# Pooling mixer of a hybrid encoder: folding counts, norm weight and scale into its matrices

## The chip, the cores and the metric

The kernel runs on one core of a Trainium2 chip. Its engines are TensorE (PE in the profile, with its weight loads as PEld), VectorE (DVE), ScalarE (ACT), GpSimd (POOL) and SyncE (SP); each takes its instructions from a queue of its own. The metric is device microseconds of one execution, lower is better.

## What is computed

Four encoder layers, each a token mixer and a SwiGLU feed-forward block with RMS norms before and after, on x of 256 tokens by 1024 channels, all in float32. The mixers are a gated convolution, a pooling mixer, attention, and a convolution again, so the order of sub-layers is conv, ffn, pool, ffn, attn, ffn, conv, ffn. The change is in the pooling mixer, whose four groups of 256 channels have windows of 2, 4, 8 and 16 tokens:

```python
def _pool_mixer(xn, w_pool, scale):
    ...
    for g, w in enumerate(POOL_WINDOWS):
        lo = jnp.maximum(t - w // 2, 0)
        hi = jnp.minimum(t + w - 1 - w // 2, s - 1)
        ...
        cnt = (hi - lo + 1).astype(jnp.float32)
        outs.append(win_sum / cnt[None, :, None] - xf[..., sl])
    p = jnp.stack(outs, axis=2)
    y = jnp.einsum('bsgc,gcd->bsgd', p, w_pool.astype(jnp.float32)).reshape(bsz, s, D_MODEL)
    return (y * scale.astype(jnp.float32)).astype(xn.dtype)

x = x + _rms(m, g[1])      # g[0] weighs the norm ahead of the mixer
```

## The kernel before

The 256 tokens are two tiles of 128 (t = 0 and 1). A float32 product is made of three matmuls of a reduced type (fp32r): every operand is split into hi, a rounded copy, and lo, the rest, and hi by hi, hi by lo and lo by hi are added up in PSUM. The split of a weight (class Weights, prep) is a ScalarE copy into hi and a VectorE subtraction into lo, in halves of 128x1024; weights come as raw tiles of 1 MB with SyncE's DMAs, three buffers deep, and up to 12 split halves are kept ahead of their use. W.pump(k) asks for k more halves at places in the program, W.get asks for one that is needed now. Activations are split the same way by split(): ScalarE copies, VectorE subtracts.

The wrapper Pinned keeps every instruction in program order on its engine, so an instruction whose data are late holds all behind it on that engine.

Each sub-layer ends in boundary(t), for one tile and then the other: ScalarE squares the result (junk) with a running sum, VectorE multiplies it by the gain of the norm behind (gpost, into mg), makes the reciprocal root (st) in small steps, adds to x, and, if the next sub-layer is not the mixer, multiplies by the gain of the norm ahead (gpre, into mg again). x_transposed(t) then transposes mg on TensorE into a PSUM bank tr and splits it into xh and xl. A feed-forward block begins with start(): a projection of tile 0 for slab 0, two steps of slab 1, x_transposed(1), the rest of slab 1, then the evacuation of both (ScalarE sg, VectorE h) and the transposes of the first h; then the projections of tile 1 follow, which need xh and xl of tile 1. A projection is 24 matmuls of 512 columns.

The gains gpost have one buffer: GpSimd issues the load of the next one when VectorE has read the last for the final time.

The pooling mixer needs no transposes ahead of it: boundary makes xh and xl in token order. pool_tables, called in run ahead of the feed-forward block before the mixer (i == 1), loads for each group a band matrix (1 in the window, minus the count on the diagonal) in two bandf buffers and casts it on GpSimd to bandr, and loads inv (one over the counts) and sc (the scale, broadcast). pool_mixer multiplies xh and xl by bandr into four PSUM banks (two of mm, two of tr), 256 columns each, with 24 calls of warm (matmuls of the identity, two instructions each, whose result nobody reads) between t = 0 and 1. Eight pieces of 128x256 are then weighted by the norm weight gc and split into ph and pl, and multiplied by the pool weight (raw tile 49) into acc: for each t, c outside and g inside. After 14 more warm calls VectorE multiplies acc by inv and sc into m, and boundary takes m.

Of the kernel before, what the change touches and what calls it, by code (L numbers as in the profile page):

```python
# [17 lines left out]
P = 128  # L18
D = 1024
# [35 lines left out]
class Weights:  # L55
# [3 lines left out]
    def __init__(self, kb, n):  # L59
        self.kb, self.n = kb, n  # L60
        self.loaded = self.prepped = self.released = 0
        self.raw, self.split, self.uses = {}, {}, {}

    def load(self):
        if self.loaded >= self.n:
# [9 lines left out]
    def prep(self):  # L75
        kb, (i, c) = self.kb, divmod(self.prepped, 2)
        while self.loaded <= i:
            self.load()
        raw = self.raw[i][:, c * 1024 : (c + 1) * 1024]
        hi = kb.wsp.tile([P, 1024], F32R, tag="hi", name=f"hi{i}_{c}")  # L80
        lo = kb.wsp.tile([P, 1024], F32R, tag="lo", name=f"lo{i}_{c}")
        n = 512 if i == 0 else 1024
        for a in range(0, 1024, n):
            sl = slice(a, a + n)
            kb.A.copy(hi[:, sl], raw[:, sl])
            kb.V.tensor_tensor(lo[:, sl], raw[:, sl], hi[:, sl].bitcast(F32), op=ALU.subtract)
        self.split[i, c] = (hi, lo)
        self.uses[i, c] = 0
        self.prepped += 1
        if c == 1:  # L90
            del self.raw[i]
            while self.loaded < min(self.n, i + 1 + NR):
                self.load()
# [16 lines left out]


class Kernel:
    def __init__(self, ctx, tc, x, w, gains, taps, pscale, lam, subg, rel, onehot, band, invc, gcol, out):
        self.tc, self.nc = tc, tc.nc
        nc = self.nc
        self.V, self.A, self.T = Pinned(tc, nc.vector), Pinned(tc, nc.scalar), Pinned(tc, nc.tensor)
        self.G, self.SP = Pinned(tc, nc.gpsimd), Pinned(tc, nc.sync)
        self.w, self.gains, self.taps, self.out = w, gains, taps, out
        self.pscale, self.lamv, self.subg, self.rel = pscale, lam, subg, rel
        self.onehot, self.band, self.invc = onehot, band, invc  # L120
        pool = lambda name, bufs=1, **k: ctx.enter_context(tc.tile_pool(name=name, bufs=bufs, **k))
        self.c = pool("c")
        self.wraw = pool("wraw", NR)
        self.wsp = pool("wsp", NP)
        self.gp = pool("gp", 1)
        self.st = pool("st", 12)
        ps = bass.MemoryType.PSUM
        self.ps_acc = pool("ps_acc", 4, space=ps)
        self.ps_mm = pool("ps_mm", 2, space=ps)
        self.ps_tr = pool("ps_tr", 2, space=ps)  # L130
        self.dram = pool("dram", 1, space=bass.MemoryType.DRAM)
        self.wi = 0
        self.W = Weights(self, w.shape[0])
        self.x = self.c.tile([P, 2, D], F32, name="x")
        xv = x.rearrange("(t p) d -> p t d", p=P)
        self.gc = self.c.tile([P, 2, 8], F32, name="gc")
        self.A.dma_start(out=self.gc, in_=gcol)
        self.gc, self.gcp = self.gc[:, 0, :], self.gc[:, 1, :]
        self.SP.dma_start(out=self.x[:, 0, :], in_=xv[:, 0, :])
        self.W.load()  # L140
        self.SP.dma_start(out=self.x[:, 1, :], in_=xv[:, 1, :])
        self.ident = self.c.tile([P, P], F32, name="ident")
        make_identity(nc, self.ident)
        self.xh = [self.c.tile([P, 8, P], F32R, name=f"xh{t}") for t in range(2)]
        self.xl = [self.c.tile([P, 8, P], F32R, name=f"xl{t}") for t in range(2)]
        self.r2 = [self.c.tile([P, 1], F32, name=f"rstd{t}") for t in range(2)]
        self.xg, self.s2 = [None, None], [None, None]
# [423 lines left out]

    def pool_tables(self, pool):

        G = self.G
        self.bandr = pool.tile([P, 4, 2, S], F32R, name="bandr")
        for g in range(4):
            bandf = pool.tile([P, 2, S], F32, tag="bandf", name="bandf", bufs=2)
            G.dma_start(out=bandf, in_=self.band[:, g])
            G.tensor_copy(self.bandr[:, g], bandf)
        self.inv = pool.tile([P, 2, 4], F32, name="inv")  # L580
        G.dma_start(out=self.inv, in_=self.invc)
        self.sc = pool.tile([P, D], F32, name="sc")
        G.dma_start(out=self.sc, in_=self.pscale[0].partition_broadcast(P))

    def pool_mixer(self, pool, g_post, g_pre, nxt):


        V, A, W, T = self.V, self.A, self.W, self.T
        wid = self.take(1)[0]
        banks = [self.mm(), self.mm(), self.tr(), self.tr()]  # L590
        spare = self.acc()
        for t in range(2):
            if t == 1:
                self.warm(spare, 24)
            for g in range(4):
                for c in range(2):
                    col = slice((2 * g + c) * P, (2 * g + c + 1) * P)
                    for k, xs in enumerate((self.xh[t], self.xl[t])):
                        T.matmul(
                            banks[g][:, c * S : (c + 1) * S], xs.rearrange("p c n -> p (c n)")[:, col],  # L600
                            self.bandr[:, g, t, :], start=t + c + k == 0, stop=t + c + k == 3,
                        )
        ph = pool.tile([P, 8, S], F32R, name="ph")
        pl = pool.tile([P, 8, S], F32R, name="pl")
        for c in range(2):
            for g in range(4):
                ch, b = 2 * g + c, banks[g][:, c * S : (c + 1) * S]
                gc = self.gcp[:, ch : ch + 1]
                A.activation(ph[:, ch, :], b, AF.Copy, scale=gc)
                V.scalar_tensor_tensor(pl[:, ch, :], b, gc, ph[:, ch, :].bitcast(F32), op0=ALU.mult, op1=ALU.subtract)  # L610
        accs = [[self.acc(), self.acc()] for _ in range(2)]
        for t in range(2):
            sl = slice(t * P, (t + 1) * P)
            for c in range(2):
                for g in range(4):
                    hi, lo = W.get(wid, g // 2)
                    o = accs[t][g // 2][:, (g % 2) * 256 : (g % 2 + 1) * 256]
                    ws = slice((2 * (g % 2) + c) * 256, (2 * (g % 2) + c + 1) * 256)
                    T.matmul(o, ph[:, 2 * g + c, sl], hi[:, ws], start=c + g % 2 == 0, stop=False)
                    T.matmul(o, ph[:, 2 * g + c, sl], lo[:, ws], start=False, stop=False)  # L620
                    T.matmul(o, pl[:, 2 * g + c, sl], hi[:, ws], start=False, stop=c + g % 2 == 2)
            for c in range(2):
                W.used(wid, c)
        self.warm(self.mm(), 14)
        for t in range(2):
            m = pool.tile([P, D], F32, tag="m", name="m", bufs=2)
            for g in range(4):
                mc = slice(g * 256, (g + 1) * 256)
                V.scalar_tensor_tensor(
                    m[:, mc], accs[t][g // 2][:, (g % 2) * 256 : (g % 2 + 1) * 256],  # L630
                    self.inv[:, t, g : g + 1], self.sc[:, mc], op0=ALU.mult, op1=ALU.mult,
                )
            self.boundary(t, [m[:, 0:512], m[:, 512:1024]], g_post, g_pre, nxt, 0 if t else None)
            if t == 0:
                self.x_transposed(0)
                W.pump(1)
# [284 lines left out]
def constants():  # L921
    rel = np.arange(-255, 257)
    n = np.abs(rel)
    bucket = np.searchsorted(np.array(BUCKET_STARTS), n, side="right") - 1 + np.where(rel > 0, 16, 0)
    onehot = (bucket[None, :] == np.arange(32)[:, None]).astype(np.float32)
    t = np.arange(S)
    band = np.zeros((4, S, S), np.float32)
    inv = np.zeros((4, S), np.float32)
    for g, w in enumerate(WINDOWS):
        lo, hi = np.maximum(t - w // 2, 0), np.minimum(t + w - 1 - w // 2, S - 1)  # L930
        cnt = hi - lo + 1
        s = t[:, None]
        band[g] = ((s >= lo) & (s <= hi)).astype(np.float32) - np.where(s == t[None, :], cnt[None, :], 0)
        inv[g] = np.float32(1) / cnt.astype(np.float32)
    inv = np.ascontiguousarray(inv.reshape(4, 2, P).transpose(2, 1, 0))
    band = np.ascontiguousarray(band.reshape(4, 2, P, S).transpose(2, 0, 1, 3))
    return onehot, band, inv


# [28 lines left out]
```

## Time and profile before

| | |
|---|---|
| median of 3 runs | 1116.5 us (1116.36 to 1116.82) |
| the profiled execution | 1116.26 us, of which the span is 1114.5 us |
| mean granted TensorE clock | 0.994 |
| busy, of the span | TensorE 98%, VectorE 62%, ScalarE 47%, GpSimd 2% |
| the first feed-forward block | starts at about 104 us |
| the pooling mixer | about 293 to 325 us |

A busy engine here is one that executes; waiting is not counted. Times within a trace are microseconds from the span's start. A row of the timeline gives start, duration, engine, line, operation, what is written from what is read, the shape, how many follow each other, and in brackets the idle time ahead of it with the engine that ended it. All instructions carry line 48, that of the wrapper, so one reads by the tiles' names.

### The profile page before, as it was taken

What the parts mean: (1) busy time and instruction counts of PE and PEld (TensorE: products, weight loads), DVE (VectorE), ACT (ScalarE), POOL (GpSimd) and SP (SyncE); (2) the same over time, 40 slices, a digit from 0 to 9 for tenths busy, and PEclk for the clock granted to TensorE, in tenths of its full rate; (3) what the DMA queues carried; (4) which work ended last, traced back from release to release, by engine and by line L of the source; (5) the groups of instructions that cost most, each with busy time, mean ns of one, the idle gap of its engine ahead of it and who ended that gap; (6) DMA issues with size and microseconds to landing.
All of it is one profiled execution on the core that took longest, in us unless ns stands there. A gap on an engine that the chain in (4) does not pass through costs nothing.

```text
span 1114.5 us, 12901 instructions
## 1 busy us (share of the span) xinstructions
PE 1089.4 (98%) x4974; PEld 886.4 (80%) x4974; DVE 692.2 (62%) x1147; ACT 529.0 (47%) x849; POOL 25.1 (2%) x45
## 2 busy tenths in 40 slices
PE   8999999999989999999998999999999999999997
PEld 6888888888868878888777778888888888888885
DVE  6867755454777554557676876455487777545443
ACT  6644544344446443445454564444355554534431
POOL 0000200000010001000000000000000000000000
PEclk9999999999989999999999999999999999999999
DMA  8754664554236557544533466454545644655421
GB/s 307 286 200 167 225 250 152 191 202 174 114 98 226 225 190 250 189 162 144 184 116 114 151 223 238 181 189 174 198 157 194 222 153 168 227 189 201 176 76 39
DMA packets 31086, 203.98 MB, mean 183 GB/s; under 512 B 3804, under 2 KB 4348, under 8 KB 7984
## 3 DMA queue, kind: packets, MB, share of 16 engines
q1 hardware_dynamic: 27216, 191.38, 46.9%
q0 software_dynamic: 3376, 11.25, 3.0%
q8 instruction: 39, 0.64, 0.2%
q10 hardware_dynamic: 432, 0.53, 0.1%
q14 instruction: 23, 0.19, 0.1%
HBM read 202.08 MB, written 2.11 MB: 183 GB/s over the span
## 4 chain that ended last, share of the span: by engine, by line
PE 90%; DVE 6%; ACT 2%; issue 1%; DMA 1%; SPq 0%; DVEq 0%; ACTq 0%
PE mm L48 58%; PE acc L48 28%; PE tr L48 4%; DVE st L48 2%; DVE lo L48 1%; DVE lg L48 1%; DVE x L48 1%; ACT hi L48 1%; ACT junk L48 1%; DVE mg L48 1%; DMA raw<-in_w 1%; ACT xh L48 1%; ACT lg L48 0%; DVE pl L48 0%; DVE xl L48 0%
## 5 line engine op out<-in xcount | busy, mean ns | idle before, releaser
L48 DVE TENSOR_TENSOR lo<-raw,hi 128x1024 fp32r<-128x1024 f32 (+1 forms) x364 | 426.0, 1219 | 64.0 <-ACT hi L48 63.3
L48 PE MATMUL mm<-hi,xh 128*128 128x512 f32 x992 | 398.5, 402 | 3.4 <-ACT hi L48 3.1
L48 PE MATMUL mm<-lo,xh 128*128 128x512 f32 x992 | 390.8, 394 | 1.7 <-DVE lo L48 1.7
L48 PE MATMUL mm<-hi,xl 128*128 128x512 f32 x992 | 391.0, 394 | 0.0
L48 ACT CAST hi<-raw 128x1024 fp32r<-128x1024 f32 (+1 forms) x364 | 359.3, 1051 | 11.1 <-DMA raw<-in_w 10.1
L48 PEld LDWEIGHTS mm<-hi,xh 128*128 128x128 f32 x992 | 187.3, 189 | 43.6 <-ACT hi L48 4.0
L48 PEld LDWEIGHTS mm<-lo,xh 128*128 128x128 f32 x992 | 187.7, 189 | 41.9 <-DVE lo L48 3.5
L48 PEld LDWEIGHTS mm<-hi,xl 128*128 128x128 f32 x992 | 187.1, 189 | 41.4 <-DVE xl L48 0.9
L48 ACT ACTIVATE sg<-mm,rstd 128x256 f32<-128x256 f32 x88 | 41.9, 476 | 362.0 <-PE mm L48 358.4
L48 DVE SCALAR_TENSOR_TENSOR h<-mm,rstd,sg 128x256 f32<-128x256 f32 x88 | 42.6, 484 | 264.7 <-ACT sg L48 264.7
L48 PE MATMUL acc<-hi,hh 128*128 128x512 f32 x352 | 117.0, 406 | 0.0
L48 PE MATMUL acc<-lo,hh 128*128 128x512 f32 x352 | 113.0, 395 | 0.0
L48 PE MATMUL acc<-hi,hl 128*128 128x512 f32 x352 | 113.0, 395 | 0.0
L48 PEld LDWEIGHTS acc<-lo,hh 128*128 128x128 f32 x352 | 66.2, 188 | 15.9
L48 PEld LDWEIGHTS acc<-hi,hl 128*128 128x128 f32 x352 | 66.1, 188 | 15.8
L48 PEld LDWEIGHTS acc<-hi,hh 128*128 128x128 f32 x352 | 63.3, 189 | 12.9 <-issue 0.9
L48 ACT ACTIVATE junk<-x 128x512 bf16<-128x512 f32 x32 | 20.2, 633 | 45.5 <-DVE x L48 45.4
L48 DVE TENSOR_TENSOR hl<-tr,hh 128x256 fp32r<-128x256 f32 x88 | 36.5, 415 | 2.3 <-ACT hh L48 2.3
L48 PEld LDWEIGHTS tr<-ident,h 128*128 128x128 f32 x176 | 24.5, 139 | 11.7
L48 PE MATMUL tr<-ident,h 128*128 128x128 f32 x176 | 33.4, 271 | 0.0
L48 ACT CAST hh<-tr 128x256 fp32r<-128x256 f32 x88 | 32.2, 366 | 2.5 <-PE tr L48 2.5
L48 ACT ACTIVATE junk<-acc 128x512 bf16<-128x512 f32 x28 | 16.7, 597 | 33.4 <-PE acc L48 33.4
(134 smaller groups left out, 636.7 us busy)
## 6 DMA issues: line engine op xcount, KB each, us to landing
raw<-in_w SPq DMA_DIRECT2D x180, 1024.0 KB, 4.8
gpost<-in_gains POOLq DMA_DIRECT2D x8, 512.0 KB, 4.1
gpre<-in_gains POOLq DMA_DIRECT2D x6, 512.0 KB, 5.0
x<-in_x SPq DMA_DIRECT2D x2, 512.0 KB, 6.3
bandf<-in_band POOLq DMA_DIRECT2D x4, 256.0 KB, 4.8
skew<-scr POOLq DMA_DIRECT2D x4, 256.0 KB, 5.4
bias<-skew POOLq DMA_DIRECT2D x4, 192.0 KB, 5.8
raw<-in_w SPq DMA_DIRECT2D x2, 256.0 KB, 4.5
```

The costliest lines, as they stand in the source:

```text
L48: r = f(*a, **k)
```

## The change

The band matrix now holds one over the count in the window, minus 1 on the diagonal, so that inv is gone; as such values are no longer exact in the reduced type, the band is split in two parts (bandh, bandl), and xh is multiplied by both, xl by bandh: 48 band matmuls in place of 32. The split is done by split(), a ScalarE copy and a VectorE subtraction for each group, where GpSimd cast. The load of sc comes first. The norm weight gcp and the scale sc are multiplied into the raw tile of the pool weight by VectorE (fold), four pieces of 128x256 for each half, ahead of that half's split. In the mixer the four PSUM banks are split whole, 128x512 each; the products go group by group; m is gone and boundary reads acc.

```diff
 # Weights.prep
         raw = self.raw[i][:, c * 1024 : (c + 1) * 1024]
+        if i in self.fold:
+            self.fold[i](raw, c)
 # pool_tables
-        self.bandr = pool.tile([P, 4, 2, S], F32R, name="bandr")
+        self.bandh = pool.tile([P, 4, 2, S], F32R, name="bandh")
+        self.bandl = pool.tile([P, 4, 2, S], F32R, name="bandl")
+        self.sc = pool.tile([P, D], F32, name="sc")
+        G.dma_start(out=self.sc, in_=self.pscale[0].partition_broadcast(P))
         for g in range(4):
             bandf = pool.tile([P, 2, S], F32, tag="bandf", name="bandf", bufs=2)
             G.dma_start(out=bandf, in_=self.band[:, g])
-            G.tensor_copy(self.bandr[:, g], bandf)
-        self.inv = pool.tile([P, 2, 4], F32, name="inv")
-        G.dma_start(out=self.inv, in_=self.invc)
-        self.sc = pool.tile([P, D], F32, name="sc")
-        G.dma_start(out=self.sc, in_=self.pscale[0].partition_broadcast(P))
+            self.split(bandf, self.bandh[:, g], self.bandl[:, g])
+
+        def fold(raw, half):
+            for j in range(4):
+                g, c = 2 * half + j // 2, j % 2
+                sl = slice(j * 256, (j + 1) * 256)
+                V.scalar_tensor_tensor(
+                    raw[:, sl], raw[:, sl], self.gcp[:, 2 * g + c : 2 * g + c + 1],
+                    self.sc[:, g * 256 : (g + 1) * 256], op0=ALU.mult, op1=ALU.mult,
+                )
+
+        self.W.fold[self.wi + 3 * NS] = fold
 # pool_mixer
-                for c in range(2):
-                    col = slice((2 * g + c) * P, (2 * g + c + 1) * P)
-                    for k, xs in enumerate((self.xh[t], self.xl[t])):
+                for k, (xs, band) in enumerate(((xh, self.bandh), (xh, self.bandl), (xl, self.bandh))):
+                    for c in range(2):
+                        col = slice((2 * g + c) * P, (2 * g + c + 1) * P)
                         T.matmul(
...
-        for c in range(2):
-            for g in range(4):
-                ch, b = 2 * g + c, banks[g][:, c * S : (c + 1) * S]
-                gc = self.gcp[:, ch : ch + 1]
-                A.activation(ph[:, ch, :], b, AF.Copy, scale=gc)
-                V.scalar_tensor_tensor(pl[:, ch, :], b, gc, ph[:, ch, :].bitcast(F32), op0=ALU.mult, op1=ALU.subtract)
+        for g in range(4):
+            f = lambda a: a[:, 2 * g : 2 * g + 2, :].rearrange("p c n -> p (c n)")
+            self.split(banks[g], f(ph), f(pl))
...
-            for c in range(2):
-                for g in range(4):
-                    hi, lo = W.get(wid, g // 2)
-                    o = accs[t][g // 2][:, (g % 2) * 256 : (g % 2 + 1) * 256]
+            for g in range(4):
+                hi, lo = W.get(wid, g // 2)
+                o = accs[t][g // 2][:, (g % 2) * 256 : (g % 2 + 1) * 256]
+                for c in range(2):
...
-            m = pool.tile([P, D], F32, tag="m", name="m", bufs=2)
-            for g in range(4):
-                mc = slice(g * 256, (g + 1) * 256)
-                V.scalar_tensor_tensor(
-                    m[:, mc], accs[t][g // 2][:, (g % 2) * 256 : (g % 2 + 1) * 256],
-                    self.inv[:, t, g : g + 1], self.sc[:, mc], op0=ALU.mult, op1=ALU.mult,
-                )
-            self.boundary(t, [m[:, 0:512], m[:, 512:1024]], g_post, g_pre, nxt, 0 if t else None)
+            self.boundary(t, accs[t], g_post, g_pre, nxt, 0 if t else None)
```

## Rows read from the trace of the kernel before

**Rows 1.** The page's busy shares: busy us, share of the span, instructions.
```profile
PE 1089.4 (98%) x4974; PEld 886.4 (80%) x4974; DVE 692.2 (62%) x1147; ACT 529.0 (47%) x849; POOL 25.1 (2%) x45
```
**Rows 2.** Timeline of TensorE behind the mixer, where the next block starts.
```profile
324.36 1.23 PE L48 MATMUL tr<-ident,mg 128*128 128x128 f32 x8 [2.26 <-DVE mg L48]
327.20 0.79 PE L48 MATMUL mm<-hi,xh 128*128 128x512 f32 x1 [1.62 <-ACT hi L48]
...
329.06 0.63 PE L48 MATMUL mm<-hi,xl 128*128 128x512 f32 x1
...
332.47 0.41 PE L48 MATMUL mm<-lo,xh 128*128 128x512 f32 x1
```
**Rows 3.** Timeline of TensorE, start of the first feed-forward block: transposes of h.
```profile
116.10 0.38 PE L48 MATMUL tr<-ident,h 128*128 128x128 f32 x2
```
**Rows 4.** Timeline of ScalarE there.
```profile
109.84 0.19 ACT L48 ACTIVATION_READ_ACCUMULATOR junk<-x 128x1 f32 x1
111.73 1.08 ACT L48 CAST xh<-tr 128x512 fp32r<-128x512 f32 x2 [1.70 <-PE tr L48]
```
**Rows 5.** Timeline of VectorE there.
```profile
114.92 0.48 DVE L48 SCALAR_TENSOR_TENSOR h<-mm,rstd,sg 128x256 f32<-128x256 f32 x1
```
**Rows 6.** Timeline of GpSimd there, and the landing times of the bandf loads.
```profile
108.71 0.54 POOL L48 DMA_DIRECT2D gpost<-in_gains  x1 [105.50 <-DVE mg L48]
109.25 0.54 POOL L48 DMA_DIRECT2D bandf<-in_band  x1
113.81 1.66 POOL L48 CAST bandr<-bandf 128x512 fp32r<-128x512 f32 x1 [4.03 <-DMA bandf<-in_band]
...
118.30 1.42 POOL L48 CAST bandr<-bandf 128x512 fp32r<-128x512 f32 x1 [2.33 <-DMA bandf<-in_band]
...
DMA to landing us min/median/max: 2.8/4.8/5.0
```
**Rows 7.** Windows there: stretch, us, POOL busy, PEclk, DMA share, GB/s.
```profile
111.00:112.00 1.00, 0.00 (x0) 1.00 1.19 274
...
122.00:123.00 1.00, 0.00 (x0) 1.00 1.06 451
```
**Rows 8.** Groups by form: count, busy us, mean ns, idle us before them.
```profile
L48 ACT CAST hi<-raw 128x512 fp32r<-128x512 f32 x4 | 2.3, 619 | 1.0 <-DMA raw<-in_w 1.0
L48 DVE TENSOR_TENSOR lo<-raw,hi 128x512 fp32r<-128x512 f32 x4 | 2.6, 689 | 1.0 <-ACT hi L48 1.0
```
**Rows 9.** Window behind the mixer: PE, PEld, DVE, ACT, POOL busy, PEclk, DMA, GB/s.
```profile
329.50:332.40 2.90, 2.90 (x8) 2.29 (x7) 1.58 (x3) 0.00 (x0) 0.00 (x0) 0.50 1.01 251
```
**Rows 10.** ScalarE's weight casts: the group until 240 us, then the timeline.
```profile
L48 ACT CAST hi<-raw x90: 614/1058/1107, 6.1 to 236.5; 128x1024 fp32r<-128x1024 f32 x86, 128x512 fp32r<-128x512 f32 x4
...
259.25 4.85 ACT L48 CAST hi<-raw 128x1024 fp32r<-128x1024 f32 x5
269.95 0.47 ACT L48 ACTIVATE sg<-mm,rstd 128x256 f32<-128x256 f32 x1 [5.85 <-PE mm L48]
...
270.57 1.06 ACT L48 CAST hi<-raw 128x1024 fp32r<-128x1024 f32 x1
275.68 0.47 ACT L48 ACTIVATE sg<-mm,rstd 128x256 f32<-128x256 f32 x1 [4.05 <-PE mm L48]
```
**Rows 11.** Timeline of VectorE at the mixer's end, t = 1.
```profile
317.36 1.66 DVE L48 SCALAR_TENSOR_TENSOR m<-acc,inv,sc 128x256 f32<-128x256 f32 x4
...
319.86 0.52 DVE L48 TENSOR_SCALAR st<-st 128x1 f32<-128x1 f32 x4 [0.25 <-ACT junk L48]
```
**Rows 12.** Timeline of TensorE in the mixer: band matmuls of t = 1, products, warm-ups.
```profile
301.23 0.38 PE L48 MATMUL mm<-bandr,xh 128*128 128x256 f32 x1 [0.73 <-ACT xh L48]
302.02 0.39 PE L48 MATMUL mm<-bandr,xl 128*128 128x256 f32 x1 [0.41 <-DVE xl L48]
...
303.85 0.28 PE L48 MATMUL acc<-hi,ph 128*128 128x256 f32 x1
...
309.76 3.29 PE L48 MATMUL mm<-ident 128*128 128x128 f32 x28
```

More of the change, by code (lines that the diff above doesn't have):

```diff
@@ L62, in __init__ @@
         self.raw, self.split, self.uses = {}, {}, {}
+        self.fold = {}
     def load(self):
@@ L112, with __init__ @@
 class Kernel:
-    def __init__(self, ctx, tc, x, w, gains, taps, pscale, lam, subg, rel, onehot, band, invc, gcol, out):
+    def __init__(self, ctx, tc, x, w, gains, taps, pscale, lam, subg, rel, onehot, band, gcol, out):
         self.tc, self.nc = tc, tc.nc
@@ L119, in __init__ @@
         self.pscale, self.lamv, self.subg, self.rel = pscale, lam, subg, rel
-        self.onehot, self.band, self.invc = onehot, band, invc
+        self.onehot, self.band = onehot, band
         pool = lambda name, bufs=1, **k: ctx.enter_context(tc.tile_pool(name=name, bufs=bufs, **k))
@@ L572, in pool_tables @@
     def pool_tables(self, pool):
-        G = self.G
-        self.bandr = pool.tile([P, 4, 2, S], F32R, name="bandr")
+        V, G = self.V, self.G
+        self.bandh = pool.tile([P, 4, 2, S], F32R, name="bandh")
+        self.bandl = pool.tile([P, 4, 2, S], F32R, name="bandl")
+        self.sc = pool.tile([P, D], F32, name="sc")
+        G.dma_start(out=self.sc, in_=self.pscale[0].partition_broadcast(P))
         for g in range(4):
@@ L594, in pool_mixer @@
                 self.warm(spare, 24)
+            xh, xl = (a[t].rearrange("p c n -> p (c n)") for a in (self.xh, self.xl))
             for g in range(4):
-                for c in range(2):
-                    col = slice((2 * g + c) * P, (2 * g + c + 1) * P)
-                    for k, xs in enumerate((self.xh[t], self.xl[t])):
+                for k, (xs, band) in enumerate(((xh, self.bandh), (xh, self.bandl), (xl, self.bandh))):
+                    for c in range(2):
+                        col = slice((2 * g + c) * P, (2 * g + c + 1) * P)
                         T.matmul(
-                            banks[g][:, c * S : (c + 1) * S], xs.rearrange("p c n -> p (c n)")[:, col],
-                            self.bandr[:, g, t, :], start=t + c + k == 0, stop=t + c + k == 3,
+                            banks[g][:, c * S : (c + 1) * S], xs[:, col], band[:, g, t, :],
+                            start=t + c + k == 0, stop=t + c + k == 4,
                         )
@@ L927, in constants @@
     band = np.zeros((4, S, S), np.float32)
-    inv = np.zeros((4, S), np.float32)
     for g, w in enumerate(WINDOWS):
         lo, hi = np.maximum(t - w // 2, 0), np.minimum(t + w - 1 - w // 2, S - 1)
-        cnt = hi - lo + 1
         s = t[:, None]
-        band[g] = ((s >= lo) & (s <= hi)).astype(np.float32) - np.where(s == t[None, :], cnt[None, :], 0)
-        inv[g] = np.float32(1) / cnt.astype(np.float32)
-    inv = np.ascontiguousarray(inv.reshape(4, 2, P).transpose(2, 1, 0))
+        inv = np.float32(1) / (hi - lo + 1).astype(np.float32)
+        band[g] = np.where((s >= lo) & (s <= hi), inv, np.float32(0)) - (s == t).astype(np.float32)
     band = np.ascontiguousarray(band.reshape(4, 2, P, S).transpose(2, 0, 1, 3))
-    return onehot, band, inv
+    return onehot, band
 def kernel(**inputs):
@@ L944 @@
     i = {k: np.asarray(v) for k, v in inputs.items()}
-    onehot, band, inv = constants()
+    onehot, band = constants()
     arrays = {
@@ L956 @@
         "band": band,
-        "invc": inv,
         "gcol": np.ascontiguousarray(i["norm_g"][0:2, 0].reshape(2, 8, P).transpose(2, 0, 1)),
```

## The prediction

> **What bounds the kernel now.** I read the page's busy shares first: TensorE is busy 98% of the span [rows 1]. The kernel is a row of matmuls with few holes, so a change is worth what it does to those holes. Next, what TensorE's matmuls wait for: at the pooling mixer the two longest waits are 2.26 us for mg and 1.62 us for a weight half, and the timeline puts both at its end, where the next feed-forward block starts [rows 2]. That is what the mixer's edits can win. The change also moves the band tables from GpSimd to ScalarE and VectorE, at the start of the feed-forward block before, around 110 us. So I read what those engines and TensorE do there [rows 3 to 6]: TensorE has no hole at all, and that is what the change can lose.
>
> **Part 1: the band tables, around 110 us.** pool_tables is called before ffn, so its instructions stand in each engine's order ahead of all of that block's. Before, only GpSimd was held: it loads a band, waits, casts it, loads the next, from 109.25 us on [rows 6], and nobody needs the result for another 180 us. After, each band is split by a ScalarE copy and a VectorE subtraction. The four copies stand on ScalarE behind the squares of the conv layer's last boundary (the last read-out ends at 109.84 + 0.19 = 110.03) and ahead of the copy xh of x_transposed(1), which starts at 111.73 [rows 4]; the four subtractions stand on VectorE ahead of xl and of h (114.92) [rows 5]. All engines keep program order, as before. So the first copy waits for a DMA that cannot be issued before gpost's (108.71, itself released by VectorE's last mg [rows 6]), and what queues behind it is xh, hi, sg on ScalarE and xl, lo, h on VectorE. TensorE waits for these: at 116.10 it is to transpose h [rows 3].
>
> When does ScalarE come free? GpSimd issues gpost at 108.71, now sc at 109.25, band 0 at 109.79 and band 1 at 110.33 (0.54 each [rows 6]). Before, band 0 was usable at 113.81, behind 512 KB of gpost. Now sc's 512 KB lie in front too. From 111 to 112 us the queues moved 274 GB/s, and they reach 451 nearby [rows 7]; 512 KB at some 340 GB/s, between these, are 1.5 us. So I take band 0 at 115.3 and band 1, 256 KB later, at 116.1. Bounds for band 0: 114.35 (sc costs nothing but its issue slot) and 116.2 (512 KB at the slower rate, and that slot). A copy of 128x512 costs 0.62 us and a subtraction 0.69 [rows 8], about 0.55 and 0.65 apart where they follow each other. There are two bandf buffers, so band 2 is issued when band 0's subtraction is done: 115.3 + 0.62 + 0.69 is about 116.6; band 3 at 117.4. The four band loads of before took 2.8 to 5.0 us to land, median 4.8; the 2.8 is band 1's, whose cast waited 2.33 us [rows 6], with nothing else moving. While ScalarE and VectorE stand still no raw buffer is released, so no weights are loaded, and I take 2.9; 5.0 is the other bound. Band 3 is then usable at 120.3 and its copy done at T = 120.95, with bounds 119.8 and 123.1.
>
> From there xh, xl, hi, lo, sg, h run as before: from xh's start (111.73) to h's end (114.92 + 0.48 = 115.40) is 3.67 us, and h was 0.70 us early for TensorE. The stall is T - 111.73 - 0.70 = T - 112.4, that is 8.5 us (7.4 to 10.7). Nothing covers it: TensorE's order has nothing else to issue. No second stall follows, as both engines' work behind xh is shifted as a whole, and slab 2, whose first half is the hi queued there, is needed only two projections (11 us) later.
>
> The Trainium skill (DMA: Bandwidth & Descriptors, Anatomy of one DMA) gives such a load a fixed 2.0 us plus its bytes at 436 GB/s, which is an estimate of 2.6 us for one band and 5.0 us for gpost, sc and band 0 together. By that rule T is 119.0, the stall 6.6 and the total 1122.9. The 2.8 us trip is near it; the median of 4.8 is not.
>
> **Part 2: the clock after that stall.** After the hole of 322.10 to 327.20, with eight transposes in it, the granted clock stood at 0.50, the 1.2 GHz level [rows 9], and 512-column matmuls came 0.427 us apart from 329.06 to 332.47 [rows 2] where 0.229 is usual: 8 matmuls, 1.6 us lost. Counted from 327.20 the slow stretch is 5.2 us, at half speed 2.6 lost. A hole of over 8 us should cost the like: I take 1.8 (1.4 to 2.6).
>
> **Part 3: the fold, and GpSimd.** Four VectorE products of 128x256 go ahead of each of the two casts of the pool weight, 1.7 us a half by the four m of the same form [rows 11]. This is raw 49, halves 98 and 99, so casts 101 and 102 (raw 0 has two casts more). Ninety casts are over by 240 us; then come 5, 1, 5, 1, so these are the last of the five at 259.25 and the one at 270.57 [rows 10]. The five end at 264.1, and ScalarE then idles until 269.95 (5.85 us idle): fold, cast and subtraction end near 269.1. The second ends near 275.3, the next sg follows at 275.68. Cost 0; without that cover each would delay an sg by up to 1.9 us. GpSimd loses four casts, one load and a wait: nothing is queued behind them until the gains of the mixer, so 0.
>
> **Part 4: the mixer.** Band matmuls grow from 32 to 48, 256 columns each, some 0.115 us apart. Those of t=0, 8 more, 0.93 us, lie ahead of the warm-ups; TensorE waited 0.73 us after these for xh at 301.23 [rows 12], and its short wait (0.26 us) among them for xl goes, since four xh products now stand first: cost 0 to 0.2. For t=1 the first four need xh alone and run before xl is there (302.02); the other 20 end at 302.02 + 20 x 0.115 = 304.3, so the products start 0.45 us after the 303.85 of before. The splits change from eight pairs of 128x256 to four of 128x512 (about 0.6 and 0.69): the last pl ends at about 305.8 instead of 306.6, each group's just ahead of TensorE. The 48 products end at about 309.9 and the 28 warm-up instructions of 3.29 us [rows 12] at 313.2. The norm chain of t=0 loses its four m and is ready nearly 1 us sooner, but the transposes wait for these warm-ups: they go from 313.36 to 313.2, a gain of 0.15.
>
> At t=1 it counts. Before: m at 317.36, then the squares, statistics at 319.86 [rows 11], transposes at 324.36. After, ScalarE squares the PSUM bank itself right behind hi, at 316.05, done at 317.6; VectorE, busy with lo until 317.2, does one mg (0.69) and starts the statistics at about 317.95. That is 1.9 us sooner; TensorE gets there at 321.95 (322.10 before), so the wait of 2.26 us shrinks to 0.5, and xh, hi and the restart at 327.20 come 1.9 us sooner too: -1.9 (-1.2 to -2.3). The late one is then the weight half, whose 1.6 us wait stays. Whether the clock still falls there is open: it would give 1.6 us back if not. With the waits for hi and lo the hole still has 2.5 us without a matmul in 4; I take it that the clock falls, and keep -1.6 for the range.
>
> **Sum.** On the profiled execution (1116.26 = span 1114.5 + 1.8, and 0.24 below the median): +8.5 + 1.8 + 0 - 1.9 = +8.4, so 1124.7; on the median 1124.9. I say 1124.8. The forecast's own range, from 7.4 + 1.4 - 3.9 to 10.7 + 2.6 - 1.2, is +4.9 to +12.1: 1121 to 1129.
>
> **Rivals.**
> The tables do not hold the queue (not slower). If the bands were there by 110 us, ScalarE's four copies would run from 110.0 to 112.2 and VectorE's from 110.4 to 113.1, and h's 0.70 us of slack would take nearly all of it: only the mixer's -1.9 is left, 1114.6, and 1113.0 if the clock stays up. It decides at the issue: the bands would have to be loaded ahead of gpost's wait. The order on GpSimd [rows 6] speaks against it. Chance 0.06, half of it within the 0.2%.
> The loads land faster. All trips like the 2.8 us one, sc hidden: T near 119.0, stall 6.6, 1122.9; chance 0.15, inside the range.
> A longer block. Both trips at 5 us or more, or the weight halves late after the restart, so that a second wait of 2 to 4 us appears at the second or third projection: 1130 to 1133. For it: the fast trip is one of four. Against: no weights load meanwhile, and all the work behind shifts together. Chance 0.1.
>
> **How the numbers follow.** Forecast 0.69, faster landing 0.15, longer block 0.1, no block 0.06. The range, 1120.5 to 1129.5, holds the first two. A measurement of this kernel can tell about 0.2% (2.2 us) from no change. Faster 0.03, same 0.04 (with a little for a stall that only balances the gain), slower 0.93.
>
> **What would show it.** In the profile after: ScalarE copies into bandh that wait for bandf until past 119 us, TensorE idle for 7 to 11 us before the transposes of h at 116 us, then 512-column matmuls 0.43 us apart at a granted clock of 0.5; GpSimd's last band load near 117 us. At the mixer: no m, squares from acc, products starting about 0.45 us later after xl, the wait for mg down to about 0.5 us. No hole at 116 us makes the forecast wrong; a hole under 5 us or over 12 makes the landing times wrong; a new gap on TensorE near 265 to 276 us makes the fold's price wrong.

## The result and the profile after

The changed kernel takes 1125.2 us (median of 4 runs, 1124.19 to 1125.55) against 1116.43 us for the one before beside it: a ratio of 1.008, 95% interval 1.0067 to 1.0092. It is slower, by 8.8 us. The profiled execution took 1124.19 us, its span is 1122.4 us, and the difference to the 1114.5 us of before, 7.9 us, can be followed through the trace in two places.

The first is the start of the first feed-forward block, the stretch of [rows 3]. The timeline of TensorE after:

```profile
124.71 0.66 PE L48 MATMUL tr<-ident,h 128*128 128x128 f32 x2 [8.50 <-issue]
...
126.02 0.63 PE L48 MATMUL mm<-hi,xl 128*128 128x512 f32 x1
126.45 0.63 PE L48 MATMUL mm<-hi,xh 128*128 128x512 f32 x1
...
128.14 0.40 PE L48 MATMUL mm<-lo,xh 128*128 128x512 f32 x1
```

Where the transposes of h followed at 116.10 before, there is now a hole of 8.50 us, and they follow 8.61 us later than before. The profile names no releaser ("issue"), so one has to ask which operand was late: h. The next seven matmuls are 0.43 us apart instead of 0.23, and the first that is followed at the usual distance again (128.14) comes 10.20 us later than the same one before (117.94). Why h was late stands in the queues of ScalarE and VectorE (where [rows 4, 5] were), and when the bands could be loaded in GpSimd's ([rows 6]):

```profile
109.64 0.19 ACT L48 ACTIVATION_READ_ACCUMULATOR junk<-x 128x1 f32 x1
114.97 1.19 ACT L48 CAST bandh<-bandf 128x512 fp32r<-128x512 f32 x2 [5.14 <-DMA bandf<-in_band]
119.79 1.25 ACT L48 CAST bandh<-bandf 128x512 fp32r<-128x512 f32 x2 [3.62 <-DMA bandf<-in_band]
120.94 1.06 ACT L48 CAST xh<-tr 128x512 fp32r<-128x512 f32 x2
...
121.68 1.28 DVE L48 TENSOR_TENSOR xl<-tr,xh 128x512 fp32r<-128x512 f32 x2
...
124.13 0.87 DVE L48 SCALAR_TENSOR_TENSOR h<-mm,rstd,sg 128x256 f32<-128x256 f32 x2
...
108.52 0.53 POOL L48 DMA_DIRECT2D gpost<-in_gains  x1 [105.30 <-DVE mg L48]
109.05 0.53 POOL L48 DMA_DIRECT2D sc<-in_pscale  x1
109.57 1.07 POOL L48 DMA_DIRECT2D bandf<-in_band  x2
116.61 1.14 POOL L48 DMA_DIRECT2D bandf<-in_band  x2 [5.97 <-DVE bandl L48]
```

ScalarE has nothing to do from 109.83 on but waits 5.14 us for the first two bands and 3.62 us for the other two; xh, for which its transposed input has lain in PSUM since about 111.7, follows at 120.94 instead of 111.73. The two pairs come from the two buffers: GpSimd issues the second pair when VectorE is done with band 0.

The second place is the mixer, which starts 10.03 us later than before (302.76 against 292.73). The timeline of TensorE before, its first band matmul and the first transposes of h in the next block:

```profile
292.73 0.28 PE L48 MATMUL mm<-bandr,xh 128*128 128x256 f32 x1
...
334.34 0.38 PE L48 MATMUL tr<-ident,h 128*128 128x128 f32 x2
```

The same after (where [rows 12] and then [rows 2] were):

```profile
302.76 0.40 PE L48 MATMUL mm<-bandh,xh 128*128 128x256 f32 x2
...
312.09 0.50 PE L48 MATMUL mm<-bandh,xl 128*128 128x256 f32 x2
...
314.47 0.28 PE L48 MATMUL acc<-hi,ph 128*128 128x256 f32 x1
...
320.16 3.29 PE L48 MATMUL mm<-ident 128*128 128x128 f32 x28
...
332.20 1.23 PE L48 MATMUL tr<-ident,mg 128*128 128x128 f32 x8 [0.22 <-DVE mg L48]
335.05 0.50 PE L48 MATMUL mm<-hi,xh 128*128 128x512 f32 x1 [1.62 <-ACT hi L48]
...
341.89 0.38 PE L48 MATMUL tr<-ident,h 128*128 128x128 f32 x2
```

The wait for mg has fallen from 2.26 to 0.22 us; the wait for the weight half is 1.62 us as it was. From the first band matmul to this restart, at 335.05, it was 34.47 us (292.73 to 327.20) and is 32.29 us, a gain of 2.18; to the first transposes of h in the next block it was 41.61 us and is 39.13, a gain of 2.48. So 10.03 - 2.48 = 7.55 us are left. The last matmul of the kernel starts 7.50 us later (1114.23 against 1106.73), so the rest of the 7.9 us, some 0.4, lies behind all matmuls, at the end of the kernel; what makes it is open.

### The profile page after: what moved, and what is told of

It reads as the page before. It is cut to its first block, busy times and chain, and to the rows that moved or that the text cites. A ratio compares the mean times of both kernels' runs of the same rounds, so it can differ in the third digit from the quotient of the medians.

```text
span 1122.4 us, 12926 instructions
## 1 busy us (share of the span) xinstructions
PE 1091.6 (97%) x4990; PEld 889.2 (79%) x4990; DVE 692.7 (62%) x1147; ACT 530.3 (47%) x849; POOL 18.9 (2%) x40
## 4 chain that ended last, share of the span: by engine, by line
PE 90%; DVE 5%; ACT 2%; issue 1%; DMA 1%; SPq 0%; DVEq 0%; ACTq 0%
PE mm L48 58%; PE acc L48 28%; PE tr L48 4%; DVE st L48 2%; DVE lo L48 1%; DVE lg L48 1%; ACT hi L48 1%; DVE x L48 1%; ACT xh L48 1%; DMA raw<-in_w 1%; DVE mg L48 1%; ACT junk L48 0%; ACT lg L48 0%; DVE xl L48 0%; DVE o L48 0%
## 5 line engine op out<-in xcount | busy, mean ns | idle before, releaser
L48 ACT ACTIVATE junk<-acc 128x512 bf16<-128x512 f32 x32 | 19.1, 597 | 34.9 <-PE acc L48 34.9
```

The costliest lines, as they stand in the source:

```text
L48: r = f(*a, **k)
```

## The experiments

Each kernel below is the changed one with the edit shown. The distance "band to h" is that from the first band matmul to the first transposes of h behind the mixer; it leaves out what happened earlier in the run. That matters, because the profiled executions also differ in what no edit touches. Those of the kernel before, of the change, of sc behind the bands, of the warm-ups and of W.pump(2) have a stretch at 1.2 GHz in the attention (588 to 592 us before, granted clock 0.57), which costs some 1.6 us; the others have none.

**The tables later.** pool_tables becomes a generator whose loads are traced behind the start of the block, and whose splits follow one by one at the end of slabs 5 to 8.

```diff
 # ffn, at the end of slab s
-            if s == 5 and tables:
-                for _ in tables:
-                    pass
+            if s >= 5 and tables:
+                if self.pool_late:
+                    next(tables, None)
...
 # pool_tables
-            self.split(bandf, self.bandh[:, g], self.bandl[:, g])
...
+        yield
+        for g in range(4):
...
+            self.split(bandf[g], self.bandh[:, g], self.bandl[:, g])
+            yield
 # run
-                        tables = iter([self.pool_tables(kp)])
+                        tables = self.pool_tables(kp, self.wi)
```

> The changed kernel with its band tables traced later: the loads right behind the start of the feed-forward block, one group's split at the end of each of slabs 5 to 8; everything else as changed. Theory (the four splits hold ScalarE's and VectorE's queues until the bands have landed): no hole of TensorE near 116 us, no stretch of 1.2 GHz behind it, so 8.5 + 1.4 us come back and the mixer's gain of some 2.2 us stays: 1114.2 us (1113.5 to 1115.0). Rival (the loss is the added work itself: eight instructions, the fold, 16 band matmuls, wherever they stand): the time stays above 1120 us, with holes at slabs 5 to 8 or at 260 to 276 us.

Measured: 1113.88 us, ratio to before 0.9978 (0.9969 to 0.9988). ScalarE and TensorE at the place of the hole:

```profile
111.75 1.07 ACT L48 CAST xh<-tr 128x512 fp32r<-128x512 f32 x2 [1.71 <-PE tr L48]
...
116.12 0.38 PE L48 MATMUL tr<-ident,h 128*128 128x128 f32 x2
```

The hole is gone, with the same added instructions in the kernel and with sc ahead of the bands as in the change. The work itself is free; its place was not. Band to h is 40.11 us (292.55 to 332.66), a gain of 1.50 on the kernel before: its restart came after the same 32.29 us as in the changed kernel, but the slow stretch behind was longer, some 12 matmuls 0.43 us apart where the changed kernel had 7. The spans of the profiled executions differ by 2.9 us (1111.6 against 1114.5). The missing stretch in the attention makes some 1.6 of it, and is no merit of the mixer. How much of the 2.3 us between the medians is of that kind, no trace shows.

**The tables on GpSimd, at the place of the change.**

```diff
-            self.split(bandf, self.bandh[:, g], self.bandl[:, g])
+            G.tensor_copy(self.bandh[:, g], bandf)
+            G.tensor_tensor(self.bandl[:, g], bandf, self.bandh[:, g].bitcast(F32), op=ALU.subtract)
```

> The changed kernel with the same place for the tables, but copy and subtraction of each band made by GpSimd. Theory (whose queue waits decides): no hole at 116 us, GpSimd's queue alone waits, until about 130 us; 1114.2 us like the later tables. Rival (the load of sc and the bands themselves delay what tile 1 needs, through DMA traffic or the buffers): the hole of several us at 116 us stays and the time is above 1120 us.

Measured: 1112.93 us in one run, no hole; band to h 40.12 us. GpSimd waits in the place of the others:

```profile
114.99 0.61 POOL L48 CAST bandh<-bandf 128x512 fp32r<-128x512 f32 x1 [4.81 <-DMA bandf<-in_band]
...
131.71 1.56 POOL L48 CAST bandh<-bandf 128x512 fp32r<-128x512 f32 x1 [2.48 <-DMA bandf<-in_band]
```

The bands land no sooner (114.99 against 114.97 us), and it costs TensorE nothing, because nothing that anyone needs is queued behind GpSimd's wait. With the run before, this leaves the queue as the cause of the hole; the transfers alone are not.

**Four buffers.** bufs=4 in place of bufs=2 for bandf.

> The changed kernel with four bandf buffers in place of two, so that all four loads are issued without waiting for a split. Theory (the stall is two trips one after the other, each mostly a fixed time to land): the second trip of about 3.2 us goes, band 3 is usable near 117.2 us, the stall falls from 8.5 to about 5.3 us, the stretch at 1.2 GHz stays, and the time is about 1122 us. Rival (the bytes set the landing: 1.5 MB behind gpost at some 300 GB/s): band 3 lands no sooner than 118.5 us, the stall stays above 6.5 us.

Measured: 1120.85 us in one run.

```profile
115.52 2.60 ACT L48 CAST bandh<-bandf 128x512 fp32r<-128x512 f32 x4 [5.12 <-DMA bandf<-in_band]
...
121.78 0.66 PE L48 MATMUL tr<-ident,h 128*128 128x128 f32 x2 [5.13 <-issue]
```

All four copies run back to back: when the first band is there, the others arrive as fast as ScalarE takes them. The hole is 5.13 us. So the stall of 8.50 us was two trips, and 3.4 us of it is the second, which two more buffers avoid. Not all of that is won: behind the shorter hole 11 matmuls come 0.43 us apart where the changed kernel has 7, which costs 2.4 us instead of 1.6. The time is 1.1 us under the expectation, and this execution is one of those without the stretch in the attention.

**sc behind the bands.** The load of sc moves below the loop over the bands.

> The changed kernel with sc loaded behind the bands, as it was in the kernel before. Theory as predicted (sc's 512 KB cost band 0 some 1.5 us on its way): band 0 usable near 113.5 us, the whole stall 1.5 us shorter, 7.0 us. Rival (sc costs its issue slot of 0.5 us only): band 0 usable near 114.4 us and a stall of 8.0 us.

Measured: 1123.84 us in one run; the hole is 7.94 us, so neither 7.0 nor quite 8.0.

```profile
109.19 0.54 POOL L48 DMA_DIRECT2D gpost<-in_gains  x1 [105.98 <-DVE mg L48]
...
117.16 0.53 POOL L48 DMA_DIRECT2D sc<-in_pscale  x1
...
114.38 1.20 ACT L48 CAST bandh<-bandf 128x512 fp32r<-128x512 f32 x2 [3.89 <-DMA bandf<-in_band]
119.23 0.62 ACT L48 CAST bandh<-bandf 128x512 fp32r<-128x512 f32 x1 [3.64 <-DMA bandf<-in_band]
120.38 0.62 ACT L48 CAST bandh<-bandf 128x512 fp32r<-128x512 f32 x1 [0.53 <-DMA bandf<-in_band]
```

Counted from gpost's issue, which differs by 0.7 us between the executions, band 0 is usable after 5.19 us instead of 6.45: sc in front cost 1.26 us, its issue included, near the 1.5 of the estimate. But sc does not vanish: it is now issued right behind the second pair, and band 3 is awaited for another 0.53 us by itself. Counted from gpost again, h is transposed 15.48 us later instead of 16.19, 0.7 us gained of the 1.5 expected. My expectation had left out that the moved load meets the second pair.

**m put back.** The later tables, but the scale is multiplied in m again, with a constant 1 where inv stood, instead of in the weight.

```diff
 # fold
+                V.tensor_scalar(raw[:, sl], raw[:, sl], self.gcp[:, 2 * g + c : 2 * g + c + 1], None, op0=ALU.mult)
...
 # pool_mixer
+            m = pool.tile([P, D], F32, tag="m", name="m", bufs=2)
+            for g in range(4):
+                mc = slice(g * 256, (g + 1) * 256)
+                V.scalar_tensor_tensor(
+                    m[:, mc], accs[t][g // 2][:, (g % 2) * 256 : (g % 2 + 1) * 256],
+                    self.one, self.sc[:, mc], op0=ALU.mult, op1=ALU.mult,
+                )
-            self.boundary(t, accs[t], g_post, g_pre, nxt, 0 if t else None)
+            self.boundary(t, [m[:, 0:512], m[:, 512:1024]], g_post, g_pre, nxt, 0 if t else None)
```

> The kernel with the tables traced later, but with the eight m products put back: the scale is not folded into the weight but multiplied in m, with a constant 1 where inv stood; counts stay in the band, the norm weight in the pool weight, the 128x512 splits and the order by groups stay. Theory (in the mixer the removed m is what counts, as it stood between the products and the squares of t = 1): the wait of TensorE for mg behind the mixer, 0.22 us without m, is 2.0 to 2.3 us again, and the time is 1.9 us above that of the later tables, 1115.8 us. Rival (the larger splits and the order by groups give the gain): the wait for mg stays under 0.8 us and the time within 0.7 us of 1113.9.

Measured: 1117.16 us, ratio to before 1.0006 (0.9997 to 1.0015). The waits behind the mixer:

```profile
320.25 1.65 DVE L48 SCALAR_TENSOR_TENSOR m<-acc,one,sc 128x256 f32<-128x256 f32 x4
...
327.24 1.23 PE L48 MATMUL tr<-ident,mg 128*128 128x128 f32 x8 [2.14 <-DVE mg L48]
330.10 0.80 PE L48 MATMUL mm<-hi,xh 128*128 128x512 f32 x1 [1.62 <-ACT hi L48]
```

The wait for mg is back at 2.14 us. From the first band matmul to the restart it is 34.77 us (295.33 to 330.10), against 32.29 without m and 34.47 before the change. So taking m away is worth 2.48 us there, and the mixer's other edits together cost 0.3 us. Band to h is 42.30 us, 2.2 us more than with the later tables. The whole difference to these, 3.3 us of the medians, is more than the 1.9 expected; the profiled execution is 2.7 us behind after its first 20 us already, with a granted clock of 0.50 around 12 to 15 us, which no edit explains, so I rest on the distances within the mixer.

**Warm-ups in the hole.** The changed kernel, with matmuls of the identity where TensorE waits for h.

```diff
             evac(0, 1, bb)
+            if self.warm_here:
+                self.warm(self.acc(), 34)
             flush(1)
...
+                    self.warm_here = i == 1
```

> The changed kernel, with 34 warm-up calls on TensorE (68 instructions, some 7.8 us) between the last matmul of slab 1 and the transposes of h, only in the block that has the band tables: they run in the hole that is there anyway. Theory (1.2 GHz behind the hole is a consequence of the idle time, worth 1.4 us): the granted clock stays at 1.00 from 116 to 130 us, the 512-column matmuls follow at 0.23 us, the first h is transposed at the same 124.7 us, and the time is 1123.8 us. Rival (those matmuls are slow for want of operands or through the engines that catch up): they stay 0.43 us apart for some 3 us, and the time stays at 1125.2 us.

Measured: 1124.21 us, ratio to before 1.0075 (1.0052 to 1.0098; 1122.58 to 1126.48 us). The times alone can't be told from the change's 1125.2; the trace can. TensorE, then two windows of this kernel (us, busy of PE, PEld, DVE, ACT, POOL, then PEclk, DMA share, GB/s):

```profile
116.20 7.75 PE L48 MATMUL acc<-ident 128*128 128x128 f32 x68
125.32 0.41 PE L48 MATMUL tr<-ident,h 128*128 128x128 f32 x2 [1.37 <-issue]
...
127.19 0.39 PE L48 MATMUL mm<-lo,xh 128*128 128x512 f32 x1
...
116.30:124.70 8.40, 7.65 (x69) 7.46 (x67) 4.48 (x7) 4.00 (x8) 1.07 (x2) 1.00 0.18 63
125.60:127.70 2.10, 2.10 (x12) 1.72 (x11) 1.01 (x3) 1.93 (x3) 0.00 (x0) 1.00 0.03 8
```

and the same windows of the changed kernel:

```profile
116.30:124.70 8.40, 0.00 (x0) 0.02 (x1) 4.86 (x9) 3.89 (x7) 1.07 (x2) 0.80 0.19 63
125.60:127.70 2.10, 2.10 (x6) 1.65 (x5) 1.37 (x2) 2.07 (x3) 0.00 (x0) 0.50 0.00 0
```

In the same 2.1 us TensorE runs 12 pieces at 1.00 or 6 at 0.50, the 1.2 GHz level. h is not transposed sooner (125.32 against 124.71 us in the change): the hole is filled, not shortened, so the slow matmuls behind the hole came from the idle time. They cost 1.6 us: from the start of the transposes to the eighth matmul behind it is 3.43 us in the changed kernel (124.71 to 128.14) and 1.87 us here (125.32 to 127.19).

**One more weight half ready.** Two forms, each on top of the later tables: W.pump(2) for W.pump(1) behind x_transposed(0), or one more W.pump(1) behind the boundary of t = 1.

```diff
                 self.x_transposed(0)
-                W.pump(1)
+                W.pump(2)
```

> The kernel with the tables traced later, and with W.pump(2) in place of W.pump(1) behind x_transposed(0) in the mixer: the weight half that TensorE waits for at the restart (1.6 us for hi and 0.5 for lo) is split one boundary earlier. Theory (that half is the last wait behind the mixer): both waits go, the statistics of t = 1 come some 1.15 us later, so the wait for mg grows from 0.2 to 1.4 us, the next half is awaited for about 0.3 us, and the hole is short enough for the clock: 1111.5 us with it, 1113.3 us if the clock falls all the same. Rival (what is saved on the half is lost on mg): 1113.9 us as before.

```diff
                 self.x_transposed(0)
                 W.pump(1)
+        W.pump(1)
```

> The kernel with the tables traced later, and with one more W.pump(1) behind the boundary of t = 1, ahead of x_transposed(1): the awaited half's cast and subtraction go ahead of the copies and subtractions of xh and xl of tile 1, which TensorE needs only a projection later. Theory: the wait for mg stays at 0.2 us, hi is ready when the transposes end, lo about 0.5 to 0.9 us later, no 1.6 us wait, and the clock stays up more likely than not: 1111.3 us, 1112.9 us if it falls. Rival (the half after next is late instead by as much): 1113.9 us as before.

Measured: 1111.2 us, ratio 0.9959 (0.9945 to 0.9973), and 1111.6 us, ratio 0.9959 (0.9948 to 0.9970). TensorE in the first and in the second:

```profile
323.37 1.23 PE L48 MATMUL tr<-ident,mg 128*128 128x128 f32 x8 [1.35 <-DVE mg L48]
...
326.23 0.50 PE L48 MATMUL mm<-hi,xh 128*128 128x512 f32 x1 [0.23 <-ACT hi L48]
327.49 0.51 PE L48 MATMUL mm<-lo,xh 128*128 128x512 f32 x1 [0.76 <-DVE lo L48]
...
330.14 0.38 PE L48 MATMUL tr<-ident,h 128*128 128x128 f32 x2
```

```profile
321.91 1.23 PE L48 MATMUL tr<-ident,mg 128*128 128x128 f32 x8 [0.22 <-DVE mg L48]
322.97 0.50 PE L48 MATMUL mm<-hi,xh 128*128 128x512 f32 x1
324.23 0.50 PE L48 MATMUL mm<-lo,xh 128*128 128x512 f32 x1 [0.76 <-DVE lo L48]
...
326.56 0.50 PE L48 MATMUL mm<-lo,xh 128*128 128x512 f32 x1 [0.68 <-DVE lo L48]
...
329.20 0.38 PE L48 MATMUL tr<-ident,h 128*128 128x128 f32 x2
```

Both beat the kernel before, by the same 0.4% within their intervals, and so the changed kernel too. In the first the wait for mg grows to 1.35 us, as expected, in the second it does not, and lo is awaited twice for some 0.7 us instead. In both the long waits are cut up, and the 512-column matmuls behind them keep their 0.23 us: band to h is 37.34 and 36.75 us, 1.8 and 2.4 us less than in the changed kernel, and 2.8 and 3.4 less than with the tables later, on which they are built. A good part of that is the clock: of the 3.4 us of the second form 1.8 come up to the restart (292.45 to 322.97, 30.52 us against 32.29), and 1.6 behind it, where the matmuls are no longer slow.

## Why the prediction was right, point by point

It named 1124.8 us, 1120.5 to 1129.5, and slower; measured were 1125.2 us.

- Part 1, the queue. As forecast in kind and size: stall 8.5 us by the sum, 8.50 us idle in the trace, and transposes 8.61 us later. Moving the splits in time or to another engine takes it away, which tells it from the work added. Band 0 was usable 6.45 us behind gpost's issue where the sum had 6.59, the second trip took 3.18 us from issue to use (116.61 to 119.79) where it had 2.9, and ScalarE was free at 120.94 where it had 120.95, in an execution that ran 0.2 us ahead: two small errors of opposite sign, so that T was met so closely is in part luck. sc's share is 1.26 us by its experiment, not 1.5. The upper bound of T, 123.1, has the slow second trip but not the late band 0 of 116.2; both together are 124.0, so the bound was too tight; no run came near it.
- The rule of the Trainium skill. By the fixed time and the rate that the Trainium skill (DMA: Bandwidth & Descriptors, Anatomy of one DMA) gives for one load, the estimates were 2.6 us for a band by itself and, with the three loads taken as one, 5.0 us for gpost, sc and band 0; from them came a stall of 6.6 and 1122.9 us. The traces have 6.45 us from gpost's issue to the use of band 0, 3.18 from the issue of the second pair, two loads together, to the use of its first band, and, with the tables on GpSimd, 3.00 for a band that nothing follows (116.92 to 119.92). The measured trips decide; the estimates were short on all three, and the time lies beyond 1122.9.
- Part 2, the clock. 1.6 us against 1.8 taken (1.4 to 2.6). That it comes from the idle time is shown by the warm-ups. That the price would be like that behind the hole of the mixer held here, but is no rule: behind the shorter hole with four buffers it was 2.4 us.
- Part 3, the fold. Shown to be covered: TensorE is 10.20 us behind the kernel before at the end of the slow stretch and 10.03 at the start of the mixer, so nothing is added in between. In the timelines of ScalarE and VectorE after (where [rows 10] was, some 10 us later):

```profile
275.01 1.67 DVE L48 SCALAR_TENSOR_TENSOR raw<-raw,gc,sc 128x256 f32<-128x256 f32 x4
...
276.76 1.05 ACT L48 CAST hi<-raw 128x1024 fp32r<-128x1024 f32 x1 [3.48 <-issue]
280.12 0.47 ACT L48 ACTIVATE sg<-mm,rstd 128x256 f32<-128x256 f32 x1 [2.31 <-PE mm L48]
...
283.06 1.05 ACT L48 CAST hi<-raw 128x1024 fp32r<-128x1024 f32 x1 [2.20 <-DVE raw L48]
285.85 0.47 ACT L48 ACTIVATE sg<-mm,rstd 128x256 f32<-128x256 f32 x1 [1.74 <-PE mm L48]
```

  The casts wait for the fold, and both are done before the next sg, which still waits for TensorE (2.31 and 1.74 us), not the other way round.
- Part 4, the mixer. -1.9 us taken (-1.2 to -2.3), -2.18 measured to the restart. The steps hold: the wait for mg 0.22 us (0.5 forecast), the products of t = 0 pushed back by the later band matmuls (314.47 is 2.38 us behind the first xl; before, 303.85 was 1.83 behind), the transposes of t = 0 set by the warm-ups, the weight half as the next to be late. The experiment with m shows that its removal gives 2.48 us and that the other edits together take 0.3 of it. Mis-sized was what comes behind the restart: the clock fell again, as taken, but for 7 matmuls instead of the 8 of before, 0.3 us of gain that the sum did not have.
- The rivals. No block: excluded by the hole. Faster landing: the second trip came near it, the first did not. A longer block, with a second wait behind the restart: not seen; the transposes of the next h follow at 132.05 without a wait.

In the profiled pair the balance is 7.9 us where the sum had 8.4; between the medians it is 8.8. The profiled execution is 1.0 us below the median of its kernel. The other executions have no trace, so what they spent it on stays open (their mean granted clock is 0.990 to 0.991, against 0.992), and that the forecast came within 0.4 us of the median is in part luck.

## What to carry to other kernels

When work moves from an idle engine to a busy one, its waits move too: price not only the instructions (here 2.5 us of ScalarE, which cost TensorE nothing at another place) but the time until their data can be there, for everything that stands behind them in that engine's order. The remedy is a place in the order, or an engine whose queue nobody needs, not less work; where neither is to be had, buffers enough to make one trip of two win part of it (here 3.4 of 8.5 us, less 0.8 for the clock). And behind the wait that a change shortens look for the next one before counting the gain: here the wait of 1.62 us for a weight half stood behind that for mg before and after the change, and cutting it up, with the slow matmuls behind it, was worth 2.8 to 3.4 us, no less than taking m away.

## What the runs showed of the hardware that was not expected

The stretch at 1.2 GHz behind a hole is no fixed price, and here it did not grow with the hole. Behind the mixer, with holes of like length, it lasted 7 matmuls in the changed kernel and 12 with the tables later (band to h 39.13 against 40.11 us), so some 1 us between kernels that differ elsewhere. Behind the hole of the tables it lasted 7 matmuls after 8.50 us and 11 after 5.13 us (four buffers). In the changed kernel the granted clock is 1.00 from 116.3 to 121.2 us and 0.50 from 121.4 to 124.7, all of it in the hole; with four buffers it is 1.00 from 116.7 to 120.1 and 0.50 from 120.3 to 121.7, where that hole ends. So the longer hole had taken in more of the slow stretch, and what of it passes in a hole costs no matmul.

GpSimd's cast of the same 128x512 took from 0.61 to 1.56 us within one execution (the tables on GpSimd), and its subtraction 1.29 to 2.15. The slow ones ran beside VectorE's weight subtractions, and these were slow too: three took 5.00 us from 124.80 on, where three take 3.50 with the tables later. The two engines are slow together, then; what they share was not tried.
